# Three edits of order and one new ending: where the last spatial mixes stand, on which engine eight small scalings run, from which pool one PSUM tile comes, and which way round the last two f-tiles are multiplied

## The chip, the core and the metric

The kernel runs on one core of one Trainium2 chip. The metric is the device time of one execution in microseconds (us); less is better. All inputs are float32. TensorE (PE) multiplies, VectorE (DVE), ScalarE (ACT) and GpSimd (POOL) work on tiles, SyncE (SP) issues nearly all DMAs. Each engine works through its own queue in order, and waits at the head of the queue for whatever the next instruction needs.

## What is computed

One layer of a hybrid decoder over 2048 prompt tokens (and 32 sample tokens): a mixer of two head groups, a cross-attention to 256 memory tokens, a gated MLP with a causal convolution, and a last norm. The reference, cut to what the change touches:

```
q, k, v, r, a, u, sv = split_cols(xn @ w_in)          # xn = rmsnorm(x, g_mix)
logg = log_sigmoid(a @ w_alpha + b_alpha) / 16        # a: 16 columns, the decay
o, S = gla_chunked(q, k, v, logg, s0)                 # gated linear attention, 4 heads
o = rmsnorm(o, g_gla_out) * silu(r)
u = gelu(u);  sv = rmsnorm(gelu(sv), g_sgu)
z = tril(w_s) @ sv + b_s                              # spatial mix, 4 heads, chunks of 128
y = concatenate([o, u * z]) @ w_out
h = x + y;  h = h + mem_attend(rmsnorm(h, g_x))
c = conv_b + sum(conv_w[j] * shifted(hn @ w_gate, j)) # hn = rmsnorm(h, g_ffn)
h = h + (gelu(c) * (hn @ w_up)) @ w_down
y_prompt = rmsnorm(h, g_final)
```

## The kernel before

**Blocks and precision.** The prompt is worked in four blocks of 512 tokens, numbered 0 to 3; 32 sample tokens ride along in the mixer of block 1 and in the MLP of block 2. Activations lie feature-major: `B.h[m]` holds 128 features by 512 tokens, `m` from 0 to 7. Every float32 product is three PE products of a high and a low part (`mm3`, lines 92 to 94), so each weight that comes by DMA is split on the core first: ACT copies the high part (`h_...`, line 84), DVE subtracts to get the low part (`l_...`, line 85, 128x1024). At the very front the memory keys and values are projected (`mkp`, `mvp`), evicted by DVE (`mkf`, line 558) and turned by PE (`mkt`, line 567).

**The order of the work.** A scheduler places the instructions of each engine; what it is given is a list of steps. `weave(main, *sides)` builds that list: each side list is spread between two indices of the main list. For a block's mixer the main list is the input projections and the first half of the output projection: `sv` at indices 0 to 4 with the decay columns `a` at 3 (`a_fn`, line 835, PSUM tile `ap`), `k`, `q`, `v` up to 10, `u` at 11 and 12, `r` (tiles `t_wr`) at 13 to 16, and from 17 the output projection's half that needs only the spatial part (`a_wo`). The side lists are the spatial gate (`sgu_steps`: statistics, one scaling per token tile, then four mixes) and the linear attention (`gla_steps`): the levels of the first head pair at 8 to 10, those of the second pair (`gla[12:]`) at 10 to 13, the gates at 16 to 18. Before, the scaling stands at 11 and the four mixes at 12 to 15, behind the levels of the second pair.

**A mix** is, for one head: four PE matmuls into `zp` (line 892), one DVE eviction with bias `z` (line 895), a product with `u` on POOL (line 905), and a split into `ch` (ACT) and `cl` (POOL, line 85), which `a_wo` then reads.

**A level** of the linear attention is a chain between engines: DVE makes a difference of cumulated decays (`e`, line 1000), ACT takes its exponential, DVE multiplies (`e` line 1016, `kr` line 1012), PE makes scores `s` (line 1022), and DVE copies the masked part into `P` (line 1026). Once all levels are in `P`, the chunk step runs on PE (`op`, `kv`, lines 1083 to 1089), with `kt` (line 1063) and the state `S` (line 1093) on DVE. `r` (line 828) is the DVE eviction of `t_wr`, and frees its PSUM bank.

**PSUM** has two pools of four banks, `acc` and `mps`; a tile waits for the reader of the one that had its bank. **The front:** `late_constants` (line 403) scales eight pieces of the decay columns (`wa`, 128x16 each) by `g_mix` on DVE.

**The end.** The MLP runs over 22 f-tiles in groups of four, and a last group of two. For the last block this last group is `down_last`: two halves of 256 tokens, in each eight feature tiles with six matmuls of 128x256, added into `B.h`; after each half, two 128-token chunks are turned (`yp`, eight PE transposes), squared on ACT, their `rstd` taken (DVE, POOL line 299), scaled on DVE (`y`, 128x512, line 1628) and stored. Ahead of it stand six pieces that turn the carried convolution columns (`conv_out_steps`, tiles `ncp`).

## Time and profile before

| what | value |
|---|---|
| three timed runs | 2852.72, 2857.22, 2857.73 us (median 2857.22) |
| the profiled execution's own time | 2855.88 us |
| its span (first to last instruction) | 2854.2 us |
| PE busy | 2823.7 us (99%) |
| DVE, ACT, POOL busy | 1775.5, 1047.8, 541.7 us |
| mean granted TensorE clock | 0.997 of full speed |

The span is what the trace's times are counted in; the execution's own time is 1.68 us longer. In the rows of a timeline the columns are the start, the duration of one or of the merged instructions, the engine, the line of the code, the operation, output `<-` inputs, shapes, the count, and in brackets how long the engine stood idle before and for whom. A PE row's duration includes the passage through the array; from one matmul to the next it is the difference of the starts. The stretches of the windows view give busy time by engine, then the granted clock (`PEclk`), then DMA.

### The profile page before, as it was taken

The numbers are of one execution on the slowest core, as the hardware profiler recorded it, in microseconds if no ns is written. First come the engines' busy times: TensorE is split into PE (matmuls) and PEld (weight loads), VectorE is DVE, ScalarE is ACT, GpSimd is POOL, SyncE is SP. The second block draws the span as 40 slices with busy tenths as digits, with TensorE's granted clock in tenths as the row PEclk, the third lists the DMA queues.
The fourth block names the chain that finished last, engine by engine and source line by source line (L and its number), as shares of the span: only waits on it lengthen the run. The fifth ranks groups of instructions, "written<-read, shape, count | busy, mean of one in ns | idle before, by whom it ended". The sixth has DMA issues, their size and how long they took to land.

```text
span 2854.2 us, 45756 instructions
## 1 busy us (share of the span) xinstructions
PE 2823.7 (99%) x17366; PEld 2460.6 (86%) x17366; DVE 1775.5 (62%) x3160; ACT 1047.8 (37%) x1942; POOL 541.7 (19%) x617
## 2 busy tenths in 40 slices
PE   8999999999999999999999999999999999999998
PEld 8888888888888888888888888899999888899998
DVE  6577468777657736555555773666666674565555
ACT  5536344333364424222124443422223543331221
POOL 1002113111110211222220021222221012131221
PEclk9999999999999999999999999999999999999999
DMA  8656679999932345877895215577776323577784
GB/s 294 215 157 200 204 232 338 340 338 338 320 108 76 97 163 183 298 270 282 318 330 186 74 54 183 192 253 257 259 264 211 104 69 118 185 256 268 271 285 175
DMA packets 363920, 625.54 MB, mean 219 GB/s; under 512 B 26730, under 2 KB 235724, under 8 KB 363702
## 3 DMA queue, kind: packets, MB, share of 16 engines
q1 hardware_dynamic: 363702, 622.62, 64.3%
q8 instruction: 138, 2.26, 0.3%
q14 instruction: 80, 0.66, 0.1%
HBM read 497.21 MB, written 125.31 MB: 218 GB/s over the span
## 4 chain that ended last, share of the span: by engine, by line
PE 96%; DVE 2%; ACT 1%; DMA 1%; issue 0%; SPq 0%; POOL 0%; DVEq 0%; POOLq 0%; ACTq 0%
PE d L92 6%; PE d L94 6%; PE d L93 6%; PE a_wo L92 2%; PE sc L94 2%; PE sc L93 2%; PE a_wo L94 2%; PE a_wo L93 2%; PE sc L92 2%; PE a_wx L93 2%; PE a_wx L94 2%; PE a_wx L92 2%; PE s L1022 2%; PE a_wg L92 1%; PE a_wup L92 1%; PE a_wg L93 1%
## 5 line engine op out<-in xcount | busy, mean ns | idle before, releaser
L92 PE MATMUL d<-acth,whi_wd 128*128 128x512 f32 (+2 forms) x720 | 244.8, 340 | 0.5 <-DVE h L1581 0.5
L93 PE MATMUL d<-actl,whi_wd 128*128 128x512 f32 (+2 forms) x720 | 242.7, 337 | 0.0
L94 PE MATMUL d<-acth,wlo_wd 128*128 128x512 f32 (+2 forms) x720 | 242.6, 337 | 0.0
L1581 DVE TENSOR_TENSOR h<-d,h 128x512 f32<-128x512 f32 (+1 forms) x232 | 133.6, 581 | 154.1 <-PE d L94 153.9
L1520 POOL TENSOR_TENSOR c<-c,bc_f 128x512 f32<-128x512 f32 (+1 forms) x88 | 138.5, 1578 | 136.4 <-ACT c L1519 135.7
L94 PEld LDWEIGHTS d<-acth,wlo_wd 128*128 128x128 f32 x720 | 135.3, 188 | 15.6 <-issue 1.6
L92 PEld LDWEIGHTS d<-acth,whi_wd 128*128 128x128 f32 x720 | 135.3, 188 | 15.3 <-issue 1.2
L93 PEld LDWEIGHTS d<-actl,whi_wd 128*128 128x128 f32 x720 | 135.4, 188 | 14.6 <-issue 1.2
L1510 ACT ACTIVATE c<-g,colsb 128x512 f32<-128x512 f32 x88 | 71.7, 815 | 204.9 <-DVE g L1479 153.4
L1542 POOL TENSOR_TENSOR c<-r_q_wup,c 128x512 f32<-128x512 f32 (+1 forms) x33 | 59.2, 1794 | 344.2 <-DVE r_q_wup L279 223.8
L92 PE MATMUL a_wo<-ch,h_wo 128*128 128x512 f32 (+1 forms) x320 | 113.6, 359 | 4.9 <-DVE r L828 4.8
L93 PE MATMUL a_wo<-cl,h_wo 128*128 128x512 f32 (+1 forms) x320 | 113.1, 354 | 0.9 <-POOL cl L85 0.9
L1507 POOL COPY carry<-g 128x2 f32<-128x2 f32 x88 | 31.1, 353 | 433.1 <-DVE g L1479 431.0
L94 PE MATMUL a_wo<-ch,l_wo 128*128 128x512 f32 (+1 forms) x320 | 113.3, 355 | 0.0
L1511 DVE SCALAR_TENSOR_TENSOR c<-g,colsb,c 128x512 f32<-128x512 f32 x88 | 86.0, 977 | 30.7 <-ACT c L1510 30.1
L92 PE MATMUL sc<-whi_qk,woh 128*128 128x512 f32 x256 | 102.1, 399 | 0.0
L93 PE MATMUL sc<-wlo_qk,woh 128*128 128x512 f32 x256 | 101.2, 395 | 0.0
L94 PE MATMUL sc<-whi_qk,wol 128*128 128x512 f32 x256 | 101.1, 398 | 0.0
L92 PE MATMUL a_wx<-pTh,whi_wx 128*128 128x512 f32 x256 | 101.1, 395 | 0.0
L93 PE MATMUL a_wx<-pTl,whi_wx 128*128 128x512 f32 x256 | 100.9, 394 | 0.0
L94 PE MATMUL a_wx<-pTh,wlo_wx 128*128 128x512 f32 x256 | 100.4, 392 | 0.0
L84 ACT ACTIVATE acth<-c 128x512 fp32r<-128x512 f32 (+1 forms) x88 | 55.9, 637 | 115.6 <-DVE c L1542 86.5
(3369 smaller groups left out, 9209.8 us busy)
## 6 DMA issues: line engine op xcount, KB each, us to landing
whi_wd<-wd SPq DMA_DIRECT2D x66, 512.0 KB
wlo_wd<-wd SPq DMA_DIRECT2D x66, 512.0 KB
r_wo<-in_w_out_dram SPq DMA_DIRECT2D x32, 512.0 KB
whi_qk<-qkd SPq DMA_DIRECT2D x32, 512.0 KB
wlo_qk<-qkd SPq DMA_DIRECT2D x32, 512.0 KB
wlo_wx<-vod SPq DMA_DIRECT2D x32, 512.0 KB
whi_wx<-vod SPq DMA_DIRECT2D x32, 512.0 KB
r_wg<-in_w_gate_dram SPq DMA_DIRECT2D x22, 512.0 KB
```

Source lines behind the costliest of these rows:

```text
L84: act.activation(hi, src, AF.Copy)
L92: pe.matmul(ps, wh, xh, start=first, stop=False)
L93: pe.matmul(ps, wh, xl, start=False, stop=False)
L94: pe.matmul(ps, wl, xh, start=False, stop=last)
L1022: pe.matmul(ps3[:, :, c * 64:(c + 1) * 64], kl[:, c * 128:(c + 1) * 128], kr3[:, :, c * 64:(c + 1) * 64], start=True, stop=True)
L1507: pool.tensor_copy(carry[:, f, :], g[:, SB:SB + 2])
L1510: act.activation(c[:, :SB], g[:, 2:SB + 2], AF.Identity, bias=cb, scale=w2)
L1511: dve.scalar_tensor_tensor(c[:, :SB], g[:, 1:SB + 1], w1, c[:, :SB], ALU.mult, ALU.add)
L1520: pool.tensor_tensor(c[:, :T], c[:, :T], B.fbc[:, :T], ALU.mult)
L1542: (dve, pool)[i].tensor_tensor(c[:, :T], q[i], c[:, :T], ALU.mult)
L1581: dve.tensor_tensor(B.h[m + mm][:, cs], ps[:, :cw], B.h[m + mm][:, cs], ALU.add)
```

## The change

1. `late_constants`: the eight scalings of `wa` run on POOL instead of DVE.
2. `a_fn`: the PSUM tile `ap` comes from `mps` instead of `acc`.
3. The spatial gate of every block: the scaling stands at main index 10 (was 11), mixes 0 and 1 at 11, mixes 2 and 3 at 12 (were 12, 13, 14, 15); so all four are in the list ahead of the second pair's last levels.
4. The end of the last block: `down_last` is replaced. `turn_h` turns `h` so that tokens lie on partitions (32 transposes, eight ACT copies into `ht`) before the last group; `last_rows` then takes the last two f-tiles with the activations as weights and the down weights as the moving side: four chunks of 128 tokens by two halves of 512 features, six matmuls of 128x512 each, added into `ht` on DVE, squared on ACT, `rstd`, scaled by DVE (line 1572), stored. For the last chunk's first half the product with `g_final` is made early on POOL and the scaling is ACT's. Four of the six `ncp` pieces move into the MLP's main list (30 to 36).

The diff, cut to its core:

```
-            dve.tensor_scalar(wa[:, k, 0:16], war3[:, k], gcol("gmix", k), None, ALU.mult)
+            pool.tensor_scalar(wa[:, k, 0:16], war3[:, k], gcol("gmix", k), None, ALU.mult)
...
-                ps = acc(f"ap{s}{ci}")
+                ps = mps(f"ap{s}{ci}")
...
-                    for k in range(2):
-                        hi, lo = acts[f0 + k]
-                        mm3(ps[:, :256], wh[:, k, ms], wl[:, k, ms], hi[:, cs], lo[:, cs], k == 0, k == 1)
-                    dve.tensor_tensor(B.h[m][:, cs], ps[:, :256], B.h[m][:, cs], ALU.add)
...
+            for c in range(4):
+                ps = mps(f"hp{c}{j}")
+                for i in range(4):
+                    pe.transpose(ps[:, i * 128:(i + 1) * 128], B.h[4 * j + i][:, c * 128:(c + 1) * 128], ident)
+                t = U(f"ht{c}{j}")
+                act.activation(t[:, :512], ps, AF.Copy)
...
+                    for k in range(2):
+                        hi, lo = acts[FT - 2 + k]
+                        mm3(ps, hi[:, cs], lo[:, cs], wh[:, k], wl[:, k], k == 0, k == 1)
+                    y = cur["ht", c, j]
+                    dve.tensor_tensor(y[:, :512], ps, y[:, :512], ALU.add)
+                    act.activation(junk, y[:, :512], AF.Square, accum_out=ss[:, j:j + 1])
+                    if c == 3 and j == 0:
+                        early = U("yg")
+                        pool.tensor_tensor(early[:, :512], y[:, :512], gfin[0][:, :512], ALU.mult)
+                dve.tensor_tensor(ss[:, 2:3], ss[:, 0:1], ss[:, 1:2], ALU.add)
+                rstd_of(ss[:, 3:4], ss[:, 2:3], 128, 1, 1.0 / D)
+                if ready:
+                    finish(*ready)
+                ready = c, ss
+            finish(*ready)
...
-        steps += weave(proj + w1, ... (sgu_st[1:nst], 11, 11), (sgu_st[nst:], 12, 15), ... (gla[12:], 10, 13), (gtail, 16, 18))
+        steps += weave(proj + w1, ... (sgu_st[1:nst], 10, 10), (sgu_st[nst:nst + 2], 11, 11), (sgu_st[nst + 2:], 12, 12), ... (gla[12:], 10, 13), (gtail, 16, 18))
...
+            sides.append((ncs[:4], 30, 36))
...
-            steps += fmain[-4:] + conv_out_steps(carry, 2, o_state_conv[0, 0], "nc") + flast
+            steps += fmain[-4:-2] + flast[:1] + fmain[-2:] + ncs[4:] + flast[1:]
```

Three places show how the engines' queues change; numbers behind names are buffer numbers, and differ between the two kernels for the same thing.

The first is DVE's queue at the front, where the memory keys are evicted (`mkf`), their turned copy stored (`mko`) and the next weights split (`l_wk`, `l_wv`). Before:

```order
L85 TENSOR_TENSOR l_wk_469<-r_wk_466,h_wk_468 128x1024
L568 COPY mko_427<-mkt_429 128x256
L568 COPY mko_428<-mkt_433 128x256
L760 COPY h_0_439<-xt_00_459 128x256
L85 TENSOR_TENSOR l_wv_475<-r_wv_472,h_wv_474 128x1024
L558 TENSOR_TENSOR mkf_480<-mkp_481,mbcs 128x256
L558 TENSOR_TENSOR mkf_480<-mkp_509,mbcs 128x256
```

And the same place of the changed kernel:

```order
L568 COPY mko_427<-mkt_429 128x256
L568 COPY mko_428<-mkt_433 128x256
L760 COPY h_0_439<-xt_00_459 128x256
L85 TENSOR_TENSOR l_wk_469<-r_wk_466,h_wk_468 128x1024
L558 TENSOR_TENSOR mkf_480<-mkp_481,mbcs 128x256
L558 TENSOR_TENSOR mkf_480<-mkp_509,mbcs 128x256
L85 TENSOR_TENSOR l_wv_475<-r_wv_472,h_wv_474 128x1024
```

Between `l_wk_469` and the two `mkf` there were three copies and `l_wv_475`; now there is nothing.

The second is ACT's queue in block 0, where the `sv` projection's four PSUM banks (`t_ws`) are read and `ap` is copied to `aT`. Before:

```order
L84 ACTIVATE h_wv_1651<-r_wv_1649 128x1024
L84 ACTIVATE qkh_1500<-qkp_1487 128x512
L84 ACTIVATE qkh_1517<-qkp_1504 128x512
L843 ACT_TABLE_LOAD
L843 ACTIVATE sv_1533<-t_ws_1240,xrs_438 128x512
```

And of the changed kernel:

```order
L841 ACTIVATE aT_1476<-ap_1477 128x512
L84 ACTIVATE qkh_1500<-qkp_1487 128x512
L84 ACTIVATE qkh_1517<-qkp_1504 128x512
L84 ACTIVATE h_wv_1651<-r_wv_1649 128x1024
L843 ACT_TABLE_LOAD
L843 ACTIVATE sv_1533<-t_ws_1240,xrs_438 128x512
```

`aT` now stands ahead of the two `qkh`, and `h_wv` behind them, directly ahead of the table load. On PE the eight `ap` matmuls stand ahead of the 24 `qkp` matmuls now, and behind the eight `wqp` transposes before.

The third is block 3, between the last scores and the output projection. PE before, from the end of the chunk step (`op`) on:

```order
L1084 MATMUL op_23500<-S_23498,qz_23406 128x128
L892 MATMUL zp_23542<-wsT,sv_22557 128x128
L892 MATMUL zp_23542<-wsT,sv_22558 128x128
L892 MATMUL zp_23542<-wsT,sv_22559 128x128
L892 MATMUL zp_23542<-wsT,sv_22560 128x128
L892 MATMUL zp_23584<-wsT,sv_22557 128x128
L892 MATMUL zp_23584<-wsT,sv_22558 128x128
L892 MATMUL zp_23584<-wsT,sv_22559 128x128
L892 MATMUL zp_23584<-wsT,sv_22560 128x128
L92 MATMUL a_wo_23665<-ch_23353,h_wo_23285 128x512
```

PE of the changed kernel, from the last scores on:

```order
L1022 MATMUL s_23431<-kr_23427,e_23423 128x2x64 x4
L1061 MATMUL ktp_23450<-ident,kh_23446 128x128 x4
L1083 MATMUL op_23491<-v_22992,P_23141 128x128
L1084 MATMUL op_23491<-S_16491,qz_23440 128x128
L1083 MATMUL op_23491<-v_22992,P_23146 128x128
L1084 MATMUL op_23491<-S_16491,qz_23442 128x128
L1089 MATMUL kv_23497<-v_22992,kt_23455 64x128 x2
L1083 MATMUL op_23502<-v_22993,P_23141 128x128
L1089 MATMUL kv_23508<-v_22993,kt_23455 64x128 x2
L92 MATMUL a_wo_23665<-ch_23227,h_wo_23309 128x512
```

DVE at the same place, before:

```order
L85 TENSOR_TENSOR l_wo_23599<-r_wo_23596,h_wo_23598 128x1024
L1085 COPY o_23069<-op_23489 128x256
L1093 SCALAR_TENSOR_TENSOR S_23509<-S_23498,ebl_23408,kv_23506 128x128
L1085 COPY o_23070<-op_23500 128x256
L895 SCALAR_TENSOR_TENSOR z_23547<-zp_23542,colsb,bsb 128x512
L895 SCALAR_TENSOR_TENSOR z_23589<-zp_23584,colsb,bsb 128x512
L298 TENSOR_SCALAR rt<-oss_23634 128x16
L828 TENSOR_SCALAR r_23608<-t_wr_23427,xrs_21831 128x512
```

And of the changed kernel:

```order
L1026 COPY_PREDICATED P_23141<-mask_147,s_23431 128x4x64
L1026 COPY_PREDICATED P_23146<-mask_147,s_23431 128x4x64
L85 TENSOR_TENSOR l_wo_23599<-r_wo_23596,h_wo_23598 128x1024
L1063 COPY kt_23455<-ktp_23450 128x512
L828 TENSOR_SCALAR r_23608<-t_wr_23463,xrs_21831 128x512
```

The eight `zp` matmuls that stood between the chunk step and `a_wo` are gone from there, and so are the two `z` evictions ahead of `r`; `a_wo` follows the first chunk steps directly, and the later chunk steps lie between its matmuls. The four `z` stand farther up in DVE's queue, two behind the `u` evictions and two ahead of the last three levels. `l_wo_23599` now stands ahead of `kt`, where before `kt` stood ahead of the split. Outside the front, these regions of the four mixers and the end, no queue changes but in buffer numbers.

More of the change, by code (lines that the diff above doesn't have):

```diff
@@ L1454, in sample_steps, with ffn_steps @@
                 + project(wo_x[0], of_o, got_o, "so"))
-    def ffn_steps(B, fin=None):
+    def ffn_steps(B, last=False):
         s, sample = B.s, B.ffn_sample
@@ L1545, in upp7, with turn_h @@
             return seven_step(*w7d["u", j], lambda: B.hn, H, use, f"wup{s}{j}")
-        def down_last(f0, half_of):
-            def step(half, ws):
-                cs = slice(half * 256, (half + 1) * 256)
-                for m in range(8):
-                    wh, wl = ws[m // 4]
-                    ms = slice((m % 4) * 128, (m % 4 + 1) * 128)
-                    ps = acc(f"d{s}{f0}{m}{half}")
-                    for k in range(2):
-                        hi, lo = acts[f0 + k]
-                        mm3(ps[:, :256], wh[:, k, ms], wl[:, k, ms], hi[:, cs], lo[:, cs], k == 0, k == 1)
-                    dve.tensor_tensor(B.h[m][:, cs], ps[:, :256], B.h[m][:, cs], ALU.add)
-            def fn(*ws):
-                for half in range(2):
-                    step(half, ws)
-                    for st in half_of(half):
-                        st.fn()
-            return Step(fn, [wready(wdd[f0, 4 * j], f"wd{s}{f0}{j}") for j in range(2)])
+        def turn_h(j):
+            for c in range(4):
[4 more added lines that the diff above has]
+                act.activation(t[:, :512], ps, AF.Copy)
+                cur["ht", c, j] = t
@@ L1595, in ffn_steps @@
                 main += [g_(j), u_(j)] + here if nf == 2 else [g_(j)] + here + [u_(j)]
-            if fin and nf == 2:
-                pend = [down_last(f0, lambda half: fin[2 * half:2 * half + 2])]
+            if last and nf == 2:
+                pend = [Step(lambda j=j: turn_h(j)) for j in range(2)]
+                pend.append(Step(last_rows, [wready(wdd[f0, 4 * j], f"wd{s}{f0}{j}") for j in range(2)]))
             else:
```

32 lines of the change are left out of this document (28 added, 4 removed).

## The prediction

> **What bounds the kernel now.** I read the page first: busy time and the chain of waits.
>
> ```profile
> PE 2823.7 (99%) x17366; PEld 2460.6 (86%) x17366; DVE 1775.5 (62%) x3160; ACT 1047.8 (37%) x1942; POOL 541.7 (19%) x617
> PE 96%; DVE 2%; ACT 1%; DMA 1%; issue 0%; SPq 0%; POOL 0%; DVEq 0%; POOLq 0%; ACTq 0%
> ```
>
> PE is the bound: it is idle for 2854.2 - 2823.7 = 30.5 us, and the change leaves its product count alone except at the end. So it can only win what PE waits for, what PE runs slowly, and the tail. The view of waits on PE says what it waited for, in total, how often, and the longest:
>
> ```profile
> PE a_wo L92 <- DVE r L828: 4.8, 4, 2.0
> PE mkt L567 <- DVE mkf L558: 3.5, 2, 2.2
> PE ap L840 <- ACT sv L843: 1.9, 1, 1.9
> PE a_wo L93 <- POOL cl L85: 0.9, 1, 0.9
> PE op L1084 <- DVE S L1093: 0.6, 1, 0.6
> ```
>
> These rows are what the four edits aim at: 11.7 us. But idle time is not the whole price. PE's timeline of block 3 shows the first `a_wo` behind its wait, and two successive ones 5.6 us later, 0.23 us from start to start:
>
> ```profile
> 2351.05 1.95 PE L892 MATMUL zp<-wsT,sv 128*128 128x128 f32 x16
> 2354.98 0.50 PE L92 MATMUL a_wo<-ch,h_wo 128*128 128x512 f32 x1 [1.98 <-DVE r L828]
> ...
> 2360.59 0.39 PE L92 MATMUL a_wo<-ch,h_wo 128*128 128x512 f32 x1
> 2360.82 0.39 PE L93 MATMUL a_wo<-cl,h_wo 128*128 128x512 f32 x1
> ```
>
> In between they are slower. Windows of the stretches behind the longest waits show why (busy time of PE, PEld, DVE, ACT, POOL; granted clock; DMA share):
>
> ```profile
> 34.00:40.00 6.00, 4.84 (x28) 4.87 (x29) 5.32 (x10) 3.00 (x5) 0.00 (x0) 0.72 1.08 370
> 1682.00:1688.00 6.00, 4.43 (x12) 3.49 (x13) 4.53 (x7) 4.52 (x8) 6.00 (x4) 0.72 0.01 3
> 2354.00:2360.00 6.00, 5.02 (x15) 3.99 (x16) 4.53 (x7) 4.74 (x7) 6.00 (x5) 0.72 0.00 0
> 108.00:116.00 8.00, 6.08 (x45) 4.10 (x44) 3.22 (x5) 7.74 (x15) 0.00 (x0) 1.00 1.05 346
> ```
>
> Three waits of about 2 us (front, block 2, block 3) are each followed by a clock of 0.72 over 6 us, which is 6 x 0.28 = 1.7 us of PE work; the wait of 1.9 us for `sv` is not (1.00). So the first three cost about 3.7 us each, not 2.
>
> [...]
>
> **Part 1, `wa` to POOL.** DVE at the front, then PE's two rows:
>
> ```profile
> 24.31 1.20 DVE L420 TENSOR_SCALAR wa<-war,colsa 128x16 f32<-128x16 f32 x8 [4.74 <-DMA war<-in_w_in_dram]
> ...
> 31.33 1.23 DVE L85 TENSOR_TENSOR l_wk<-r_wk,h_wk 128x1024 fp32r<-128x1024 f32 x1 [1.15 <-ACT h_wk L84]
> ...
> 33.47 1.21 DVE L85 TENSOR_TENSOR l_wv<-r_wv,h_wv 128x1024 fp32r<-128x1024 f32 x1
> 34.60 0.74 DVE L558 TENSOR_TENSOR mkf<-mkp,mbcs 128x256 f32<-128x256 f32 x2
> ```
>
> ```profile
> 32.70 0.28 PE L94 MATMUL mkp<-mh,l_wk 128*128 128x256 f32 x1
> 35.16 0.43 PE L567 MATMUL mkt<-ident,mkf 128*128 128x128 f32 x2 [2.18 <-DVE mkf L558]
> ```
>
> DVE stood 4.74 us for `war`, with `mkf` behind it. Without that wait the copies run before `l_wk`, and `mkf` follows `l_wk` directly. `l_wk` itself waits for ACT and a DMA, so it stays at 31.33 to 32.56; `mkf` then starts near 32.7 and `mkt` near 33.2 instead of 35.16. PE's second stall shrinks by about 1.9 us, and the clock should not fall behind the 0.4 left: 1.9 + 1.7 = 3.6, taken as 3.5 us. The first stall (3.5 - 2.18 = 1.3 us) shortens too, but I count nothing: PE meets the DMA of the same weights next. Bounds 0.5 (the copies turn out late) and 4.3. The eight POOL scalings have no row; whether they cost 0.15 us each as on DVE or several times that, POOL's queue is otherwise empty there and `ap` comes 70 us later.
>
> **Part 2, `ap` from the other pool.** ACT around the wait, and `ap` itself:
>
> ```profile
> 108.11 1.06 ACT L84 ACTIVATE h_wv<-r_wv 128x1024 fp32r<-128x1024 f32 x1 [4.54 <-DMA r_wv<-in_w_in_dram]
> 109.08 1.29 ACT L84 ACTIVATE qkh<-qkp 128x512 fp32r<-128x512 f32 x2
> 110.39 1.28 ACT L843 ACT_TABLE_LOAD   x1
> 111.68 2.42 ACT L843 ACTIVATE sv<-t_ws,xrs 128x512 f32<-128x512 f32 x4
> ```
>
> ```profile
> 112.42 1.92 PE L840 MATMUL ap<-h,wa 128*32 128x512 f32 x16 [1.92 <-ACT sv L843]
> 114.28 0.50 PE L92 MATMUL a_wk<-xh,h_wk 128*128 128x512 f32 x1
> ```
>
> `ap` waited for the bank that the first `sv` frees. Now `ap` (1.86 us) goes ahead of `qkp`, and `a_wk` needs that bank. PE is through with `qkp` and `wqp` 1.86 us later than before (112.3), so `qkh` comes later too: about 111.5, then `h_wv` 112.6, the table load 113.9, `sv` 114.5. `a_wk` starts near 114.6, not 114.28: the wait moves and is not shorter, +0.3 us. At 2.3 us it is also longer than the three behind which the clock fell, so I add 1.6: +1.9. Bounds: 0.5 less (ACT no later) and 2.2 more.
>
> **Part 3, the mixes.** DVE in block 3, around the chunk step and at its end:
>
> ```profile
> 2337.11 1.42 DVE L1026 COPY_PREDICATED P<-mask,s 128x256 f32<-128x256 uint8 x4
> 2339.17 0.69 DVE L1063 COPY kt<-ktp 128x512 f32<-128x512 f32 x1 [0.64 <-PE ktp L1061]
> 2339.78 1.22 DVE L85 TENSOR_TENSOR l_wo<-r_wo,h_wo 128x1024 fp32r<-128x1024 f32 x1
> ...
> 2352.15 1.64 DVE L895 SCALAR_TENSOR_TENSOR z<-zp,colsb,bsb 128x512 f32<-128x512 f32 x2 [0.47 <-PE zp L892]
> ...
> 2354.19 2.71 DVE L828 TENSOR_SCALAR r<-t_wr,xrs 128x512 f32<-128x512 f32 x4
> ```
>
> `a_wo` waited for `r`, behind two `z`. Those go: in blocks 2 and 3 that returns 2.0 + 1.7 = 3.7 us each. What is late next: the last scores end, two `P` take 0.7 us while PE turns `ktp` (0.45), so PE waits 0.35 for `op`; then `l_wo` (1.22) and `kt` (0.69) stand between PE and `kv`, which is ready 2.7 us behind the scores where PE is there at 1.25: 1.45. `r` then costs 0.25. At the end the gates' `ch`, `cl` come directly ahead of the last `a_wo`: about 0.5. Sum 2.5 us, in pieces that should leave the clock alone: 3.7 - 2.5 = 1.2 us saved in each, bounds 3.7 saved and 1 lost.
>
> Block 1 has the rest: 0.9 (`cl`), half of what is left of `r` (4.8 - 2 x 1.98 = 0.8), and hand-overs around them, an estimate of 2 in all; its output projection lies between the chunk steps now, so I count 1.5 saved (bounds 0.5 and 2.5). In block 0 the other half for `r` goes, and the 0.6 for `S` stays: 0.4.
>
> **Part 4, the end.** The last down matmul and the outputs turned behind it, ACT's first square of the outputs, and the last steps of POOL and DVE:
>
> ```profile
> 2843.47 0.28 PE L94 MATMUL d<-acth,wlo_wd 128*128 128x256 f32 x1
> 2843.59 1.32 PE L1621 MATMUL yp<-ident,h 128*128 128x128 f32 x8
> ```
>
> ```profile
> 2836.81 0.60 ACT L1622 ACTIVATE junk<-yp 128x512 bf16<-128x512 f32 x1 [27.14 <-PE yp L1621]
> ```
>
> ```profile
> 2848.93 0.54 POOL L299 TENSOR_TENSOR yss<-rt,neghalf 128x1 f32<-128x1 f32 x1 [1.78 <-DVE rt L298]
> 2849.51 1.41 DVE L1628 SCALAR_TENSOR_TENSOR y<-yp,yss,gf 128x512 f32<-128x512 f32 x2 [0.66 <-POOL yss L299]
> ```
>
> Before, 96 matmuls of 128x256 (0.12 from start to start, 11.5 us) and 16 of the 32 transposes (0.11, by the sixteen `zp` of the same shape in 1.95 us: 1.8) precede the end of the last down matmul: 13.3. Now it is 48 of 128x512 (0.23, 11.0) and all 32 transposes (3.5): 14.5, so it ends 1.2 later, near 2844.95. But no transpose and no PE follow. The tail is then an add (0.7, half of the `y` pair), a square (0.6), two small DVE steps (0.3), POOL 0.55, the chunk before's `y` pair (1.4) on DVE's queue, one `y` (0.7) and hand-overs (0.5): 4.75, against 2850.92 - 2843.75 = 7.2 before. 2.4 - 1.2 = 1.2 us saved; bounds 0 and 2.5. The last store is of the same size. The eight ACT copies (0.6 each) lie in the 27.14 us in which ACT has nothing else; were they late, the adds would wait, at most 0.6.
>
> **The sum**, against the profiled execution's 2855.88 us (span plus 1.68): -3.5 + 1.9 - 0.4 - 1.5 - 1.2 - 1.2 - 1.2 = -7.1 us. The median of the runs stands 1.34 above that execution; I take the difference to the median: 2857.22 - 7.1 = 2850.1 us, 0.25% less. About 0.2% (5.7 us) is what a measurement of this kernel can tell from no change.
>
> **Rivals.** *Nothing comes in the place of the waits.* `kt` and the gates are in time, the clock never falls: front 4.0, `ap` nothing, block 0 0.4, block 1 2.5, blocks 2 and 3 3.7 each, end 2.0: 16.3 us, 2840.9. For it: DVE is busy 62% overall; against it: `l_wo` stands ahead of `kt` in the new queue.
>
> *The waits move and keep their length.* The new 1.8 us around `op` and `kv` pull the clock down as 1.98 did; then blocks 2 and 3 give 3.7 - 2.5 - 1.6, about nothing, the front keeps its clock loss (-1.9), `ap` costs 1.9, and blocks 0 and 1 and the end give 2: 2 us, 2855.2. For it: the threshold lies somewhere between 1.92 and 1.98 in these rows.
>
> *POOL holds DVE back in the mixers.* DVE's `e`, free and beside POOL's `cl`:
>
> ```profile
> 2323.15 0.68 DVE L1000 TENSOR_TENSOR e<-b 128x512 f32<-128x512 f32 x1
> ...
> 2325.99 1.78 DVE L1000 TENSOR_TENSOR e<-b 128x512 f32<-128x512 f32 x1
> ```
>
> ```profile
> 2325.73 1.48 POOL L85 TENSOR_TENSOR cl<-z,ch 128x512 fp32r<-128x512 f32 x1 [0.74 <-ACT ch L84]
> ```
>
> `e` ends 0.56 behind `cl`, as if it had started only then: 1.1 us lost. Two products and two `cl` (5.2 us on POOL) now lie beside the last three levels, where PE has eight `zp` and 41 products between one score and the next (10.3 us), and DVE two `l_wo`, four `P`, two `z`, two `e` and two `kr` (about 7.5 by such rows): 3 us of slack. Fully held, DVE is 2.2 us late; with the 2.5 above and a clock loss of 1.6 that is 6.3 us per block against 3.7, 3.7, 2 and 0.4 removed: 15.4 us lost; with 4.7 won at front and end and 1.9 lost at `ap`, +12.6, 2869.8. It decides from 3.5 us of hold on, where the kernel is 0.2% slower; I expect half the 5.2. [...]
>
> **How the numbers follow.** Forecast 0.47, nothing in place 0.17, waits kept 0.25, POOL's hold 0.11. The forecast's own bounds reach from about -11 to -3, three quarters of it below -5.7. Faster by over 0.2%: 0.17 + 0.36 + 0.02 = 0.55; within: 0.11 + 0.22 = 0.33; slower: 0.12. The range, 2841 to 2858, takes in the first three cases and leaves out POOL's hold and a little at the other end.
>
> **What would show it.** Right: in the changed profile `mkt` waits under 1 us near 33, with a clock of 1.00 at 34 to 40; `a_wk` waits over 2 us near 114; `a_wo` no longer waits for `r` by 2 us in blocks 2 and 3, and instead `kv` waits for `kt` by 1 to 2; the last down matmul ends later relative to the span's end by 2.4 less. Wrong: a clock of 0.72 behind new waits in the mixers, scores that wait for `kr`, or new waits between 35 and 100 that give the front's gain back.

## The result and the profile after

| kernel | median of runs | lowest to highest | ratio to before |
|---|---|---|---|
| before, on the same chip | 2854.97 us (4 runs) | 2852.60 to 2857.73 | |
| changed | 2876.64 us (4 runs) | 2874.16 to 2879.33 | 1.0077, 95% interval 1.0066 to 1.0089 |

The change makes the kernel 0.8% slower, by about 22 us. The forecast was 7 us less; the result lies outside its range, on the side to which it gave 0.12.

First the page of the changed kernel, busy time and the chain:

```profile
PE 2833.6 (99%) x17318; PEld 2463.0 (86%) x17318; DVE 1784.5 (62%) x3143; ACT 1057.1 (37%) x1955; POOL 556.9 (19%) x626
...
PE 93%; DVE 4%; ACT 1%; issue 1%; DMA 0%; POOL 0%; SPq 0%; POOLq 0%; DVEq 0%; ACTq 0%
```

The span is 2874.8 us, 20.6 more than before. PE is idle 41.2 us (30.5 before) and busy 9.9 us longer, with 48 products fewer (the new end does the same work in half as many, each twice as long: 0.23 us from start to start instead of 0.12): so half of the loss is waiting and half is PE running slowly, as behind the waits of before. DVE's share of the chain has doubled. What PE waited for now (total, times, longest):

```profile
PE s L1022 <- DVE kr L1012: 10.6, 7, 2.3
PE ktp L1061 <- POOL kh L1058: 4.0, 3, 1.6
...
PE a_wk L92 <- ACT sv L843: 2.3, 1, 2.3
...
PE kv L1089 <- DVE kt L1063: 1.4, 2, 0.9
...
PE a_wo L92 <- ACT ch L88: 0.9, 2, 0.5
PE mkt L567 <- DVE mkf L558: 0.8, 1, 0.8
```

The row for `r` (4.8 us before) is gone, `mkt` fell from 3.5 to 0.8. In their place stands what the prediction named as a sign that it is wrong: scores that wait for `kr`, 10.6 us, and `ktp` that waits for `kh`, the next step of the same chain.

Where the span was lost shows when PE's stages end, changed minus before: at the start of block 0's `a_wq` 0.0 us; over the mixers (from the last `t_wv` product to the end of `a_wo`) of blocks 0 to 3 it is 13.5, 0.5, 1.9 and 4.6; behind the last output projection 0.7. The mixers are all of it, and block 0 alone two thirds. There, PE's last scores of the second pair, and `ktp` behind them, before:

```profile
242.49 1.05 PE L1022 MATMUL s<-kr,e 128*128 128x128 f32 x8
...
245.23 1.06 PE L1022 MATMUL s<-kr,e 128*128 128x128 f32 x8
...
247.75 1.05 PE L1022 MATMUL s<-kr,e 128*128 128x128 f32 x8
...
251.21 0.60 PE L1061 MATMUL ktp<-ident,kh 128*128 128x128 f32 x4
```

Between these rows stand products of `t_wr`, and no score has a bracket, so none waited. The changed kernel, same place, nothing left out:

```profile
255.92 0.40 PE L94 MATMUL t_wr<-h_wr,xl 128*128 128x512 f32 x1
258.67 1.13 PE L1022 MATMUL s<-kr,e 128*128 128x128 f32 x8 [2.35 <-DVE kr L1012]
260.97 2.04 PE L1022 MATMUL s<-kr,e 128*128 128x128 f32 x8 [1.18 <-DVE kr L1012]
265.16 2.04 PE L1022 MATMUL s<-kr,e 128*128 128x128 f32 x8 [2.14 <-DVE kr L1012]
268.11 1.11 PE L1061 MATMUL ktp<-ident,kh 128*128 128x128 f32 x4 [0.91 <-POOL kh L1058]
```

The three levels stand back to back: four waits, 6.6 us, and the same eight matmuls take 2.04 instead of 1.05. The windows of the changed kernel (busy time by engine, granted clock, DMA) show it:

```profile
34.00:40.00 6.00, 6.00 (x52) 6.00 (x53) 6.00 (x12) 3.41 (x7) 0.00 (x0) 1.00 1.06 369
...
260.00:272.00 12.00, 7.97 (x29) 6.83 (x30) 9.46 (x19) 3.10 (x6) 1.70 (x1) 0.57 0.14 44
```

A clock of 0.57 over 12 us here, and 1.00 at the front, where before had 0.72. DVE of the changed kernel just ahead of those scores, and POOL beside it:

```profile
251.94 1.11 DVE L1000 TENSOR_TENSOR e<-b 128x512 f32<-128x512 f32 x1
252.97 2.32 DVE L85 TENSOR_TENSOR l_wof<-r_wof,h_wof 128x1024 fp32r<-128x1024 f32 x1
255.22 1.51 DVE L1016 TENSOR_TENSOR e<-e,k 128x256 f32<-128x256 f32 x1
256.65 1.87 DVE L1012 SCALAR_TENSOR_TENSOR kr<-e,sel,q 128x256 f32<-128x256 f32 x2
258.44 0.68 DVE L1000 TENSOR_TENSOR e<-b 128x512 f32<-128x512 f32 x1
259.61 0.43 DVE L1016 TENSOR_TENSOR e<-e,k 128x256 f32<-128x256 f32 x1 [0.48 <-ACT e L1002]
259.95 0.88 DVE L1012 SCALAR_TENSOR_TENSOR kr<-e,sel,q 128x256 f32<-128x256 f32 x2
```

```profile
250.37 3.84 POOL L905 TENSOR_TENSOR z<-z,u 128x512 f32<-128x512 f32 x2 [21.60 <-DVE z L895]
254.18 3.67 POOL L85 TENSOR_TENSOR cl<-z,ch 128x512 fp32r<-128x512 f32 x2
```

Beside POOL's products and `cl`, `e` takes 1.11 instead of 0.68, the split 2.32 instead of 1.2, the second `e` 1.51 instead of 0.42 and `kr` 1.87 instead of 0.88: 3.6 us. So POOL's hold is real, but it explains the first of the four waits. Behind 257.9 POOL is through and DVE at its usual pace, and PE goes on waiting: one level takes DVE and ACT some 2.4 us (from the start of `e` at 258.44 to the end of `kr` at 260.83), and PE has nothing else in its queue.

The rows of waits for `kr` and `kh` have other places too. In block 0 the first level of the second pair waits as well, behind `u`, the first two mixes and 24 products. In blocks 2 and 3 the last three levels don't wait at all; what waits there is the second level of the pair (1.26 and 1.27 us) and `ktp` (1.59 and 1.50). Block 0's first level, and the two waits of block 3:

```profile
229.10 1.16 PE L1022 MATMUL s<-kr,k 128*128 128x128 f32 x8 [2.18 <-DVE kr L1012]
...
2337.89 1.13 PE L1022 MATMUL s<-kr,e 128*128 128x128 f32 x8 [1.27 <-DVE kr L1012]
...
2365.32 0.66 PE L1061 MATMUL ktp<-ident,kh 128*128 128x128 f32 x4 [1.50 <-POOL kh L1058]
```

The other thing to see is on ACT. It loads a table, 1.28 us each, when it goes from `e` to `u` or back: in block 0 of the changed kernel at 219.86 and 230.48 ahead of `u`, at 223.75 and 232.94 ahead of `e`. In e2, which gives `u` the function of `e`, the groups of 5.1 us and more have four loads at L1005 and none at L833 or L1002. The groups of table loads, of before and of the changed kernel:

```profile
L833 ACT ACT_TABLE_LOAD x6 | 7.7, 1283 | 7.1 <-DVE u L832 7.1
...
L1005 ACT ACT_TABLE_LOAD x5 | 6.4, 1283 | 0.1
L1002 ACT ACT_TABLE_LOAD x5 | 6.4, 1283 | 0.1
```

```profile
L1005 ACT ACT_TABLE_LOAD x8 | 10.3, 1283 | 3.3 <-DVE e L1004 3.2
L833 ACT ACT_TABLE_LOAD x8 | 10.3, 1283 | 7.2 <-DVE u L832 7.1
...
L1002 ACT ACT_TABLE_LOAD x4 | 5.1, 1283 | 0.1
```

16 loads became 20. In each of blocks 0, 2 and 3 there are two more, since levels and `u` evictions are now mixed on ACT, which they were not before; in block 1, where they were, there are two fewer.

### The profile page after: what moved, and what is told of

Read it like the earlier page. It is cut to its first block, busy times and chain, and to the rows that moved or that the text cites. A ratio compares the mean times of both kernels' runs of the same rounds, so it can differ in the third digit from the quotient of the medians.

```text
span 2874.8 us, 45679 instructions
## 1 busy us (share of the span) xinstructions
PE 2833.6 (99%) x17318; PEld 2463.0 (86%) x17318; DVE 1784.5 (62%) x3143; ACT 1057.1 (37%) x1955; POOL 556.9 (19%) x626
## 4 chain that ended last, share of the span: by engine, by line
PE 93%; DVE 4%; ACT 1%; issue 1%; DMA 0%; POOL 0%; SPq 0%; POOLq 0%; DVEq 0%; ACTq 0%
PE d L92 6%; PE d L93 6%; PE d L94 6%; PE a_wo L92 2%; PE a_wo L93 2%; PE a_wo L94 2%; PE sc L94 2%; PE sc L93 2%; PE sc L92 2%; PE a_wx L93 2%; PE a_wx L94 2%; PE a_wx L92 2%; PE a_wg L92 1%; PE a_wg L93 1%; PE a_wup L93 1%; PE a_wup L92 1%
## 5 line engine op out<-in xcount | busy, mean ns | idle before, releaser
L92 PE MATMUL d<-acth,whi_wd 128*128 128x272 f32 (+1 forms) x688 | 235.8, 343 | 0.0
L93 PE MATMUL d<-actl,whi_wd 128*128 128x272 f32 (+1 forms) x688 | 233.7, 340 | 0.0
L94 PE MATMUL d<-acth,wlo_wd 128*128 128x272 f32 (+1 forms) x688 | 233.5, 340 | 0.0
L94 PEld LDWEIGHTS d<-acth,wlo_wd 128*128 128x128 f32 x688 | 129.3, 188 | 15.8 <-issue 1.6
L92 PEld LDWEIGHTS d<-acth,whi_wd 128*128 128x128 f32 x688 | 129.4, 188 | 14.7 <-issue 1.2
L93 PEld LDWEIGHTS d<-actl,whi_wd 128*128 128x128 f32 x688 | 129.4, 188 | 14.4 <-issue 1.2
L1511 DVE SCALAR_TENSOR_TENSOR c<-g,colsb,c 128x512 f32<-128x512 f32 x88 | 86.3, 981 | 30.5 <-ACT c L1510 30.0
```

The lines of the kernel that those rows point to most:

```text
L92: pe.matmul(ps, wh, xh, start=first, stop=False)
L93: pe.matmul(ps, wh, xl, start=False, stop=False)
L94: pe.matmul(ps, wl, xh, start=False, stop=last)
L1511: dve.scalar_tensor_tensor(c[:, :SB], g[:, 1:SB + 1], w1, c[:, :SB], ALU.mult, ALU.add)
```

## The experiments

Four theories are told apart. A: POOL's work beside DVE's levels holds the chain back. B: the table loads between `u` and `e` do. C: mixes 2 and 3 stand in the way of the last levels in DVE's queue. D: the levels of the second pair come too late in the list. Runs e1 to e4 were made on one chip, then e5 to e8, e9 to e12 and e13 to e15. Runs e2 to e5 and e9 leave out or change part of the computation, as their expectations say, to see what its time is. Of e2 to e5 and e9 there is a single time each; the kernel before itself spread from 2850.75 to 2860.19 us over 19 runs on one chip, so a difference of 2 or 3 us between single times says nothing. The medians of before differ by up to 1.9 us from chip to chip, which is also in every difference from the changed kernel's 2876.64 us below.

The mixers' loss against before in each run (last `t_wv` product to the end of `a_wo`, us), to which the sections below refer:

| run | block 0 | block 1 | block 2 | block 3 |
|---|---|---|---|---|
| changed kernel | 13.5 | 0.5 | 1.9 | 4.6 |
| e1, mixes as before | 0.2 | 1.1 | -0.2 | -1.5 |
| e4, POOL small | 6.3 | 2.1 | 0.7 | 1.0 |
| e5, POOL small, no table loads | 7.1 | 2.1 | -1.6 | -1.2 |
| e6, mixes 2 and 3 at 14 | 4.7 | 10.3 | 3.1 | 5.1 |
| e9, e5 with block 0's mixes 2 and 3 at 14 | -0.7 | 3.4 | -1.4 | -1.2 |
| e10, scaling 11, mixes at 12 | -0.2 | 0.2 | -3.5 | -3.1 |
| e13, levels earlier | 12.4 | 11.5 | 11.0 | 7.5 |
| e14, e10's mixes, old `ap` and end | -0.2 | 0.2 | -3.5 | -3.1 |

Each number compares two single profiles, and in blocks 2 and 3 of the one of before the clock fell. e8, e11 and e12, whose mixers are in the order of before, differ from it by up to 0.2 us in block 0, 4.0 in block 1 and 1.8 in blocks 2 and 3; a difference of that size can be the clock's alone.

**Is it part 3, and by which of its means: e1 to e4.** Part 3 taken back in the changed kernel:

```
-(sgu_st[1:nst], 10, 10), (sgu_st[nst:nst + 2], 11, 11), (sgu_st[nst + 2:], 12, 12)
+(sgu_st[1:nst], 11, 11), (sgu_st[nst:], 12, 15)
```

> The changed kernel with part 3 alone undone (scaling at 11, mixes at 12 to 15); parts 1, 2 and 4 stay. If the mixers are where the 22 us went (trace: block 0 +13, blocks 2 and 3 +2 and +4), this is back within 4 us of before, 2853 to 2859. If the other parts share in the loss, it is above 2862.

Measured 2854.04 us (10 runs) against 2853.79: 1.0001 (0.9991 to 1.0011). The whole loss is part 3; parts 1, 2 and 4 together are worth nothing that can be measured.

```
-act.activation(o, o, AF.Gelu_apprx_tanh)
+act.activation(o, o, AF.Exp)
```

> The changed kernel with the activation of u an exponential instead of the GELU, so that ACT does not switch tables between u and the levels' exponentials in the mixers (u is wrong; all four engines keep the order of their other instructions). Theory A (POOL holds DVE): at most 3 us less than the changed kernel, 2873 to 2877. Theory B (ACT's table loads of 1.28 us, two more in block 0 and in block 2 and 3 each in front of the exponentials, make the levels late): 8 us less or more, below 2869.

2871.34 us, 5.3 below the changed kernel and between the two ranges: the four more loads, and those that stood there before, cost a part. In its trace no score of blocks 2 and 3 waits any more, while `ktp` there still waits 1.6 and 1.5 us.

```
-pool.tensor_tensor(z[:, :T], z[:, :T], B.u[h][:, :T], ALU.mult)
-split(hi[:, :T], lo[:, :T], z[:, :T], pool)
+pool.memset(z[:, :T], 1.0)
+act.activation(hi[:, :T], z[:, :T], AF.Copy)
+pool.memset(lo[:, :T], 0.0)
```

> The changed kernel with the mixes' POOL work replaced by fills: z is set to 1 and cl to 0 by POOL, in place of z times u and of z less ch (the spatial part of the output is left out; the instructions stand at nearly the same places). POOL stays in the chain, but reads nothing. Theory A (POOL's reads hold DVE's operations with two inputs): DVE's kr, e and l_wof no longer take 1.4 to 2.8 us, and the time falls by 8 us or more, below 2869. Theory B (table loads) and theory C (the order alone, the levels simply stand too late): within 4 us of the changed kernel.

2868.74 us, 7.9 less. Beside the memsets DVE keeps its own pace (`e` 0.42 and 0.68, the split 1.23): with POOL only writing, 0.5 us at a time, no hold shows.

```
-pool.tensor_tensor(z[:, :T], z[:, :T], B.u[h][:, :T], ALU.mult)
-split(hi[:, :T], lo[:, :T], z[:, :T], pool)
+pool.tensor_tensor(z[:, :16], z[:, :16], B.u[h][:, :16], ALU.mult)
+act.activation(hi[:, :T], z[:, :T], AF.Copy)
```

> The changed kernel with the product z times u on 16 of 512 columns and no low part (ch is read twice; the rest of the product and the low part are left out), so that POOL does almost nothing in the mixes; the order shifts a little more than in the run with fills. Theory A: 8 us less or more, below 2869, like the run with fills. Theory C (order): above 2870.

2866.70 us, 9.9 less; e3 lies within the spread of it. A and B both find something, and neither comes near the 22 us: with hardly any work on POOL, block 0 still loses 6.3 us. `ktp` of blocks 2 and 3 waits in neither e3 nor e4. But their edits also moved ACT's steps: both have 26 table loads for `u` and `e`, against 20, so these times may make POOL's part too small.

**Both together, mixes 2 and 3 later, two other parts alone: e5 to e8.** e5 has the edits of e2 and e4.

> The changed kernel with both: POOL's product on 16 columns and no low part, and the exponential in place of the GELU of u (both leave out or change the spatial part). If POOL's hold (9.9 us in the run with little POOL work) and the table loads (5.3 us) are separate and were all of it, 2861 or less by their sum and the rest, some 7 us over before, is the order alone (theory C). If they are two sides of the same lateness, about 2866; if the order alone costs nothing, 2857 or less.

2864.22 us: 12.4 together, not the sum of 15.2. Blocks 2 and 3 now lose nothing, though PE has only 3, 6 and no products after the first, second and third of their last levels. Block 0 keeps 7.1, and its longest wait is longer than any in the changed kernel, with DVE at its usual pace (`e` 0.42 and 0.68, `kr` 0.88): between the last two `kr` DVE has a split (1.22 us) and two pairs of `P` (0.76 each) to do, and PE has no product. PE's row in e5:

```profile
257.44 2.05 PE L1022 MATMUL s<-kr,e 128*128 128x128 f32 x8 [3.06 <-DVE kr L1012]
```

So in block 0 something else than A and B holds the scores.

```
-(sgu_st[nst + 2:], 12, 12)
+(sgu_st[nst + 2:], 14, 14)
```

> The changed kernel with mixes 2 and 3 at index 14 instead of 12: in DVE's queue their two z stand behind the last levels' e and behind kt, no longer ahead of the last three levels; mixes 0 and 1 stay ahead of the levels. Theory C (two z that wait for PE's zp stand at the head of DVE's queue while the last three levels could run): the waits of the scores behind 250 us in block 0 go, and most of the loss with them, 2855 to 2863. Theory A (POOL beside DVE, wherever the mixes stand) and theory B (the table loads come with u): above 2866.

2880.58 us (4 runs), 1.0089 (1.0074 to 1.0105): not what C said. Block 0 gains 9 us, block 1 loses 10. C is a part of block 0's loss at most, and no cure. PE's queue changed as well: in block 0 it has 2, 4 and 20 products after the first, second and third of the last levels, where the changed kernel has none; in block 1 five levels now stand back to back, and the scores wait 3.5 and 1.7 us. PE's waits in e6:

```profile
PE s L1022 <- DVE kr L1012: 10.4, 7, 3.5
PE a_wo L92 <- DVE r L828: 5.7, 3, 2.6
```

The old wait for `r`, and one of 4.5 us in three for `cl`, are back beside the new one for `kr`.

e7 is the kernel before with part 1 and the mixes closer together; e8 is the kernel before with the new end.

```
-(sgu_st[nst:], 12, 15)
+(sgu_st[nst:], 12, 14)
```

> The kernel before with wa on POOL and the mixes at 12 to 14 (were 12 to 15): mix 1 joins mix 0 ahead of the last three levels, the first three levels stay ahead of u. If what hurts in the changed kernel is that u and z stand ahead of the first levels of the second pair, nothing of that comes back here: 2849 to 2855. If a second z and its POOL work ahead of the last three levels are enough to hurt, 2857 or more.

2857.03 us (10 runs), 1.0007 (0.9997 to 1.0016): nothing that can be told from before. The median lies in the second range, but not for its reason: in the profile no score of the mixers waits, and what grew is the wait for `r` in blocks 2 and 3, 2.87 us instead of 1.98.

> The kernel before with the new end alone (part 4). By the prediction 1.2 us less than before, 2852 to 2854; by the trace of the changed kernel, whose span ends 0.6 us later from the last attention product on, 0 to 1 us more than before.

2855.79 us (10 runs), 1.0002 (0.9993 to 1.0011): nothing.

**Block 0, the order, parts 1 and 2 alone: e9 to e12.** e9 is e5 with mixes 2 and 3 later in block 0 only:

```
-(sgu_st[nst + 2:], 12, 12)
+(sgu_st[nst + 2:], 12 if s else 14, 12 if s else 14)
```

> The run with little POOL work and the exponential for u (2864.2), and in block 0 alone mixes 2 and 3 at index 14, so that their two z stand behind the last levels there. If the 7 us that were left in block 0 are DVE standing at the head of its queue for zp while the last three levels could run (theory C, in block 0), they go: 2855 to 2860. If they are the first levels of the second pair standing behind u and z, they stay: 2862 or more.

2855.83 us: the 8.4 us that A and B leave are gone, and no score in block 0 waits. With A, B and C taken away together the loss is gone; with one or two of them, part of it. The edit also changes PE's queue in block 0, which now has 2, 4 and 20 products after the last three levels, where e5 has none, so C and the bare places aren't told apart here. This reads like slack: each eats from the same store, and the loss begins when it is empty. e10 asks for the store itself. In the changed kernel only the place of the scaling and the mixes is altered, so that the first levels of the second pair stay ahead of the mixes:

```
-(sgu_st[1:nst], 10, 10), (sgu_st[nst:nst + 2], 11, 11), (sgu_st[nst + 2:], 12, 12)
+(sgu_st[1:nst], 11, 11), (sgu_st[nst:], 12, 12)
```

> The changed kernel with the scaling at 11 and all four mixes at 12: the first three levels of the second pair stay ahead of u, as before the change, ACT switches its table no more often, and all four z stand between u and the last three levels, r directly behind kt. Theory D (what costs is the first levels behind u and z, with the table loads): 2850 to 2856, the waits for r gone. Theories A and C (POOL's work and the z that wait for zp ahead of the last three levels): 2862 or more.

2851.45 us (10 runs), 0.9991 (0.9982 to 1.0000): 25 us below the changed kernel, with all four mixes still ahead of the last levels, and all of POOL's work there. DVE of e10 in block 3:

```profile
2327.93 2.96 DVE L1012 SCALAR_TENSOR_TENSOR kr<-e,sel,q 128x256 f32<-128x256 f32 x2
2330.82 1.78 DVE L1000 TENSOR_TENSOR e<-b 128x512 f32<-128x512 f32 x1
```

`kr` takes more than three times its 0.88 and `e` 1.78 instead of 0.68: the hold is as strong as in the changed kernel, where `kr` takes up to 2.84 in block 0. But PE's scores behind it hardly notice:

```profile
2332.39 1.06 PE L1022 MATMUL s<-kr,e 128*128 128x128 f32 x8
...
2334.55 1.13 PE L1022 MATMUL s<-kr,e 128*128 128x128 f32 x8 [0.39 <-DVE kr L1012]
...
2337.59 1.05 PE L1022 MATMUL s<-kr,e 128*128 128x128 f32 x8
...
2341.51 0.60 PE L1061 MATMUL ktp<-ident,kh 128*128 128x128 f32 x4
```

Over the whole kernel it is this row:

```profile
PE s L1022 <- DVE kr L1012: 1.3, 3, 0.6
```

The table loads are back at 16, as before. What differs besides is the order of PE's queue. Counted from it, the matmuls of the second pair's stretch (`s`: four rows are one level; each `t_wr` product, 0.23 us from start to start where its row says 0.40, is work that waits for no level):

| kernel, block | PE's queue up to `ktp` |
|---|---|
| before, 0 | s8 t_wr20 s8 vop12 t_wr7 zp4 t_wr41 **s4** t_wr8 **s4** t_wr7 **s4** t_wr11 ktp |
| changed, 0 | zp8 t_wr24 s4 t_wr24 s8 t_wr22 s4 vop12 zp4 t_wr2 zp4 t_wr24 **s4 s4 s4** ktp |
| e10, 0 | s8 t_wr20 s8 vop12 t_wr7 zp12 t_wr10 zp4 t_wr37 **s4** t_wr5 **s4** t_wr7 **s4** t_wr10 ktp |
| before, 2 and 3 | s8 a_wu3 s4 a_wu13 t_wr14 s4 zp4 t_wr34 **s4** t_wr6 **s4** t_wr7 **s4** t_wr12 ktp |
| changed, 2 and 3 | zp8 a_wu21 t_wr13 s4 t_wr5 s4 t_wr19 s4 t_wr6 s4 zp8 t_wr41 **s4** t_wr3 **s4** t_wr9 **s4** ktp |
| e10, 2 and 3 | s8 a_wu3 s4 a_wu13 t_wr14 s4 zp12 t_wr4 zp4 t_wr43 **s4** t_wr3 **s4** t_wr9 **s4** t_wr13 ktp |

In the changed kernel the mixes come at index 11, ahead of the first levels, which move behind them and the `u` evictions. The `t_wr` products, of which there are 96 in a block, are spent between those first levels; once the last three begin there are none left in block 0, and none ahead of `ktp` in blocks 2 and 3. There PE waits, and at the first levels, which now stand behind `u` and its table loads. Between the last three levels of blocks 2 and 3 the changed kernel and e10 have the same 3 and 9 products, and no score waits there by more than 0.4 us in either: what counts is whether the chain is ready when PE arrives, not a number of products per level. (`zp4` ahead of the last levels shows that mix 0 stood there before the change too.)

e11 and e12 are the kernel before with part 1 alone (`dve.tensor_scalar(wa...` to `pool.tensor_scalar(wa...`) and with part 2 alone (`acc(f"ap...` to `mps(f"ap...`).

> The kernel before with wa on POOL alone (part 1). By the prediction 3.5 us less than before (the second wait for mkf and the clock loss behind it). If the front's gain is lost to a later wait of the same length, as the changed kernel's trace has it at the start of the q projection (0.0 us), within 1 us of before.

2852.50 us (10 runs), 0.9993 (0.9984 to 1.0003).

> The kernel before with ap from the mps pool alone (part 2). By the prediction 0.3 us more by the queue and 1.6 by the clock that falls behind a wait of 2.3 us: 1.9 more than before, with a clock under 1.00 near 114. If the bank was the wait, as the edit has it, about 2 us less.

2855.85 us (10 runs), 1.0004 (0.9995 to 1.0014). Both on the side forecast, neither separable from nothing.

**Theory D, and the best of it: e13 to e15.** If the first levels' place is what matters, moving the levels forward in the changed kernel should help too:

```
-(gla[12:], 10, 13)
+(gla[12:], 10, 11)
```

> The changed kernel with one pair of numbers changed: the second pair's levels at 10 to 11 instead of 10 to 13, the mixes where the change has them. In DVE's queue the first levels then stand ahead of u again, and the last three between the two pairs of z. Theory D (the levels' place): 2850 to 2857. If the mixes at 11 and 12 cost by themselves, 2865 or more.

2896.78 us (4 runs), 1.0143 (1.0129 to 1.0157): 20 us worse than the changed kernel. D falls as it was put, and so do the table loads as the reason here: there are 16 of them, as before. PE's waits in e13, and one of block 0's last scores:

```profile
PE s L1022 <- DVE kr L1012: 14.1, 8, 7.6
PE ktp L1061 <- POOL kh L1058: 7.2, 4, 2.5
```

```profile
236.69 2.05 PE L1022 MATMUL s<-kr,e 128*128 128x128 f32 x8 [7.61 <-DVE kr L1012]
```

Earlier is not better. In blocks 0, 2 and 3 the last three levels and `ktp` stand back to back here (in block 1 nine products stand after the first of them, none after the others), and the `t_wr` products that could have covered them come behind (21 after the chunk step's start in block 0, none between the levels). What helps is neither early nor late levels but independent products for PE where the chain isn't ready yet.

e14 is the kernel before with part 1 and the mixes at 12; e15 is that with the new end.

> The kernel before with wa on POOL and the mixes at 12 (parts 2 and 4 left out). By the runs so far: 2.6 us for wa, about 4 for the waits for r of blocks 2 and 3 with the clock losses behind one of them, no clock loss at a_wk: 2847 to 2851.

2849.89 us (11 runs), 0.9982 (0.9973 to 0.9990): better than both kernels, 5 us below before. The waits for `r` are gone and blocks 2 and 3 give 3.5 and 3.1 us, near the 3.7 that the prediction says they are worth. Half of that is the clock's fall in the profile of before: against e11, in whose blocks 2 and 3 the clock did not fall, it is 1.7 us each.

> The same with the new end. By the spans behind the last attention product in the traces with the new end (0.7 to 1.6 us more than before) 1 us more than without it; by the prediction 1.2 us less.

2851.82 us (11 runs), 0.9987 (0.9978 to 0.9996). The new end is no gain on this base either. The two intervals against before overlap, but the eleven times of e15 set beside the eleven of e14 on the same chip are on average 1.9 us longer, with a standard error of 0.6: here it costs time.

## Why the prediction was wrong

**Part 3, the failed step.** Its sum of what would be late next (2.5 us a block) has `op`, `kv`, `r` and the gates, and puts the scores and `ktp` at nothing. The reason stands in the third rival: PE has "eight `zp` and 41 products between one score and the next (10.3 us)", and DVE so "3 us of slack". That is one stretch, ahead of the first of the last three levels, and for blocks 2 and 3 it was right: none of these scores waits there. The waits came where no slack was counted. The first levels behind `u` wait 2.18, 1.26 and 1.27 us in blocks 0, 2 and 3; `ktp`, with no product ahead of it, 0.91, 1.59 and 1.50; and in block 0 the last three levels, back to back, 5.67. With 0.23 in block 1 that is the 14.6 us of the waits for `kr` and `kh`. The clock fell with them: in the mixers it took 10.2 us of PE's work, and 3.4 before.

In blocks 2 and 3 neither the hold nor the bare places did this alone. With the place of the mixes altered (e10) the hold stays and the loss goes; with POOL's work and the table loads nearly gone (e5) the bare places stay, and the loss goes too. By the traces the loads make an early level late there (the second level's wait is gone in e2; in e3 and e4, with two more loads in each of these blocks, the third waits 1.9 and 1.7 us), and POOL's work makes `ktp` late (its wait is there in e2, and gone in e3 and e4). In block 0 the loss is partly there without either, 7.1 us in e5.

Two things fed this error. Only block 3's order was read, and taken for all four: in block 0, forecast at a gain of 0.4, the loss is 13.5. And of the first levels only their new place was seen, not that they take the `t_wr` products with them, nor that ACT then changes its table four times more. By e2 the loads' share is about 5 us, by e4 POOL's 10, by e5 against e9 that of the mixes and the bare places in block 0 is 8. These are no parts of one sum: both together give back less than the sum of each (e5), e4 has six more loads, and each is a difference of single times.

What the prediction said would be late next was there in size: `op` waits 0.7 us in two (0.35 each forecast), `kv` for `kt` 1.4 in two (1.45 each forecast, so half), `a_wo` for `ch` 0.9 in two (0.5 each). And the gain was there to be had: forecast "nothing in place" 3.7 us in blocks 2 and 3, of which 1.7 are the clock's, e14 shows 3.5 and 3.1, again with the clock's part of before.

**The rival with the right sign.** "POOL holds DVE back in the mixers" gave 2869.8 us and comes nearest, but for the wrong places: 6.3 us in every block, where two thirds of the loss lie in block 0 and 0.5 in block 1. Hold enough was there: in block 0 alone 3.6 us beside the last levels, and 4.0 beside the first (`kr` 2.84, the split 2.31 and an `e` of 128x256 1.38, instead of 0.88, 1.22 and 0.43). The second two products and their `cl` took 7.5 us on POOL in block 0 and 6.7 in block 3, where the prediction has 5.2. What the hold cost depended on whether PE had products there. e3, in which POOL only writes and DVE isn't slowed (the split 1.23, `e` 0.42, against 2.32 and 1.51 beside POOL's products and `cl`), gave back nearly what e4 did, 7.9 against 9.9 us. By what means POOL holds DVE no run shows.

**The clock.** The prediction read a fall of the clock behind each wait of 1.98 us or more and priced it at 1.6 to 1.7 us. Other runs of the same code show that it is not so fixed. The same waits for `r`, 1.98 us, in e11 and in e12 (windows behind them in blocks 2 and 3):

```profile
1681.00:1687.00 6.00, 5.40 (x23) 4.42 (x24) 4.53 (x6) 4.63 (x7) 6.00 (x4) 1.00 0.01 3
2350.00:2356.00 6.00, 5.33 (x23) 4.34 (x24) 4.53 (x6) 4.71 (x7) 6.00 (x4) 1.00 0.00 0
```

```profile
1686.00:1692.00 6.00, 5.34 (x16) 4.25 (x17) 4.53 (x6) 4.69 (x7) 6.00 (x4) 0.72 0.02 4
2357.00:2363.00 6.00, 5.20 (x22) 4.24 (x23) 4.52 (x7) 4.74 (x7) 6.00 (x5) 1.00 0.00 0
```

Not at all in e11, once in e12 and in e1, twice in the profile of before and in e8: six of ten. The wait of `a_wk` for `sv`, 2.29 or 2.30 us in each of eleven profiles that have part 2, is followed by 0.72 in seven and by 1.00 in four. The term should have been a chance of about 0.6 times 1.7 us. That the runs of one kernel spread over 9 us may have the same cause; e8's profiled run, 4.4 us above its median, has a clock of 0.58 over 8 us from 914 and from 972 us, where before, one microsecond earlier in the same code, has 1.00. Why the clock falls behind one wait and not behind another of the same length no run shows, and no length between 1.92 and 1.98 us divides the cases, as the rival of the kept waits had it.

**Part 1.** The mechanism was right: `mkt` waits 0.79 us, and the clock at 34 to 40 is 1.00. The size, 3.5 us, was too large: the front ends (start of the first `t_ws` product) 2.0 to 2.2 us earlier in the changed kernel, e1, e11 and e14, and e11 is 0.9993 of before. The wait varies by itself: with the old front it is 2.18 us in before, 1.93 in e8 and 0.96 in e12, so part of the agreement is luck. The clock's 1.7 was the chance of one execution: e8 and e12 have the old front, and both show 1.00 at 34 to 40; their fronts end 1.3 and 1.7 us ahead of the profiled one of before. Against those, `wa` on POOL is worth about 0.5 us.

**Part 2.** Right as a mechanism and in its length. The changed kernel's row:

```profile
112.70 0.50 PE L92 MATMUL a_wk<-xh,h_wk 128*128 128x512 f32 x1 [2.30 <-ACT sv L843]
```

It starts 1.6 us sooner than before, where the front ends 2.2 sooner: 0.6 later by its own stage, forecast 0.3. Alone it costs +0.8 us by the medians, and both nothing and the forecast 1.9 (1.0007) lie in e12's interval.

**Part 4.** Wrong in the tail. From the last `dr` product on, in the changed kernel:

```profile
2864.45 2.41 DVE L1572 SCALAR_TENSOR_TENSOR y<-ht,yss,gf 128x512 f32<-128x512 f32 x2
...
2864.61 1.70 POOL L1591 TENSOR_TENSOR yg<-ht,gf 128x512 f32<-128x512 f32 x1 [0.77 <-DVE ht L1587]
...
2864.79 0.40 PE L94 MATMUL dr<-whi_wd,actl 128*128 128x512 f32 x1
...
2866.85 0.68 DVE L1587 TENSOR_TENSOR ht<-dr,ht 128x512 f32<-128x512 f32 x1
...
2870.57 0.75 DVE L1572 SCALAR_TENSOR_TENSOR y<-ht,yss,gf 128x512 f32<-128x512 f32 x1 [0.66 <-POOL yss L299]
```

The last add was priced as starting at once. It stands behind a pair of `y` on DVE, and that pair takes 2.41 us beside the early product `yg` on POOL (1.70), where the next pair, at 2868.24, takes 1.41. From the end of the last product (2865.2) to the end of the last `y` (2871.3) it is 6.1 us, not 4.75; the 1.4 us are the start of that add. Counted from the last attention product, the last down product ends 1.4 us later (forecast 1.2), and behind it the span ends 0.8 sooner (forecast 2.4): the end costs 0.7 us in this profile instead of saving 1.2.

**What stays open.** Why block 1 lost so little in the changed kernel and 10 us in e6 was read from the waits and from PE's queue (3, 6 and 19 products after the last three levels in the changed kernel, five levels back to back in e6), not tried. In block 0 it isn't told apart what the mixes cost in DVE's queue and what the bare places cost on PE, since each edit that moved the one moved the other. How the loss divides among POOL, the tables and the mixes can't be said closer than the single times allow.

## What to carry to other kernels

When a step is moved in a list that a scheduler turns into queues, follow each chain between engines link by link, in every block, before and after the move: when is the link ready, and has the bounding engine independent work until then? Slack counted over one stretch of one block hides an empty place elsewhere. What moves past the chain may cost little itself and still cost much through the cover that others lose: the scaling and the first two mixes one index later were worth 25 us here (e10). A clock loss that one profile shows behind a wait is a chance, to be counted over several profiles before it goes into a sum.

## What the runs showed of the hardware

- The same wait, in the same code, may or may not pull the clock down (above): seven of eleven times behind 2.29 or 2.30 us, six of ten behind 1.98 us.
- POOL's operations on equal tiles vary too beside DVE's: the second two products with `u` in block 0 took 3.84 us and their two `cl` 3.67, the first pairs 2.74 and 2.69.
- POOL's memsets were not in DVE's way (e3): beside them `e` took 0.42 and 0.68 us and the split 1.23, as when alone, where beside POOL's products and `cl` in the changed kernel they took 1.51, 1.11 and 2.32. The memsets are short (0.53 us each), and it is one profile.
- In the profiles of before and of the changed kernel the granted clock falls to 0.50 and to no other value (0.50 over 261 to 271 us of the changed one); ahead of PE's last product a fall lasts 3.41 us six times, 6.83 once and 10.24 once. In the windows of 2 us of e2 to e9 none goes below 0.50, and e2 has one of about 13.6 us (256 to 270). The 0.72 over 6 us is one such fall of 3.41 us, 1.7 us of PE's work; the others are two, three and four times that.
